# A product that begins inside the attention in front of it: three attentions of a three-block kernel on one Trainium2 core

## The chip, the cores and the metric

The kernel runs on one core of a Trainium2 chip. The engines are TensorE (PE, matmuls; PEld its weight loads), VectorE (DVE), ScalarE (ACT), GpSimd (POOL) and SyncE (SP, which issues most DMAs). The metric is the device time in microseconds; before the change the median of three runs is 1748.19 us (1746.01 to 1751.26).

## The reference

Batch 1, 512 tokens, width 1024. A first block, then a second block of two layers; in all three there is an attention whose output, gated, goes through a 1024 × 1024 product:

```python
# first block ("layer 0" in the change's words): differential attention, 8 heads
y_attn = rms_norm(diff_attention(q, k, v, lam)) @ w_attn_branch
y_mem  = memory_cross_attention(q_m, rms_norm(mem, norm_mem), w_mem_kv) @ w_mem_branch
mix = gates[0] * y_attn + gates[1] * y_pool + gates[2] * y_mem
x = x + rms_norm(mix @ w_out);  x = x + rms_norm(convolved_gated_ffn(x))
# second block, even layer: 16 heads over 512 tokens + 256 context tokens
y_lat = concat([oa * silu(ag), ob * silu(bg)]) @ ev_w_out
# second block, odd layer: a conformer convolution (31 taps, layer norm) beside
# neighbourhood attention of 8 heads
y_lat = concat([conv * silu(cg), od * silu(dg)]) @ od_w_out
```

Every matrix product is made in three matmuls of rounded halves (high × high, high × low, low × high), which gives close to float32.

## The kernel before

Activations lie with features on the partitions, as eight blocks of 128 × 512 (high halves `h`, low halves `l`). A `Product` (L451) is one output tile: 128 output features, with `kt` steps (8 for a width of 1024), each three matmuls (`mm3`, L446) over one block k of the input. Its weights come by one DMA on SP's queue (`load`), one cast on ScalarE (`whi`) and one subtraction on VectorE (`wlo`).

Products are kept in batches in one queue. `step(batch)` (L343) does the next step of the product that is current, whichever batch it is of, and takes the next product when one is done; `fetch` loads weights ahead. What is called later in time on the other engines is put off by `defer(us, fn)`: a clock of planned TensorE microseconds (`on_pe`, `tick`) says when it is emitted. TensorE's instructions stay in the order in which they are emitted; those of the other engines may be moved by the framework's scheduler, by their readiness.

An attention is a list of items, each scores, transposes ("turns") and, for every second one, an output; `attention` (L637) strings them with a lead of two or three items, and between its functions steps of a batch are put: `weave` (L406) with a fixed number per function, `pace` (L422) with so many that the batch ends with the items. The three places:

- Layer 0: `weave` at L1037 puts steps of the batches in the queue (`diffs`, the queries, keys and values of the heads, then `gates0`, three gate products) between the functions, 2.4 each (`DR`), until `gates0` is done. Then `steps(branches, KD)` (L1039) does the eight steps of the next product, gate 3 (`branch_gate(32, 3)`), `flush()` emits what is put off, and the batch `branches` goes on with branch 0 (`w_ab`, reading the attention's output `ao`, one head per block), gate 4, branch 1 and so on. Beside them runs `modulation(1, ...)`, weight rows on VectorE (L863).
- Second attention, L1603 to L1620: the filler (query and gate products) is woven with 0.5 steps per function (`LR`), one less for each product (`LZ`), 4 at once at the start; sixteen steps (`LA`) come ahead of it. Each pair of heads gives one block of `mix`: `lat_apply` multiplies it with its gate, and 2.5 us later (planned) it is split. The PSUM banks are 1 for products and 3 for the attention during the items, 2 and 2 after (`set_banks`). The product `outs` (L1612) comes after `run(filler)` and `flush()`; its result is added to `x` (`residual`), which is loaded again there (`open_x`).
- Last attention, L1819 to L1830: `pace` with gate, convolution and head products; blocks 4 to 7 of `mix` are from the attention (`na_gated`), 0 to 3 from the convolution (`conv_gated`), whose taps run on VectorE in the background. `outs` (L1824) is made after `pace`.

The memory's root: the sum of squares of `mem` is reduced by a matmul, the inverse root computed by nine small instructions on VectorE (`rsqrt`), and a matmul broadcasts it (`spread`), `gap` planned us after the sums (`SumSq.rms`, L591, called at L783). It scales the memory's keys and values when they leave PSUM (`rooted`, L705).

Of the kernel before, what the change touches and what calls it, by code (L numbers as in the profile page):

```python
# [42 lines left out]
LA, LR, LZ = 16, 0.5, 1.0  # L43
# [158 lines left out]
def body(nc, tc, A, out, dbg=None):  # L202
# [98 lines left out]
    def flush():  # L301
        while deferred:
            heapq.heappop(deferred)[2]()
# [39 lines left out]
    def step(batch):  # L343

        if current[0] is None:
            if not ahead:
                fetch()
            if batch.pulled and not batch.left:
                return END
            if not ahead[0].ready():  # L350
                return True
            ahead[0].parts()
            ahead[0].low()
            current[:] = [ahead.pop(0), 0]
        p, k = current
        fetch()
        last = k == p.kt - 1
        current[:] = [None, 0] if last else [p, k + 1]
        p.batch.steps -= 1
        p.step(k)  # L360
        if last:
            p.batch.left -= 1
            fetch()
        tick()
# [57 lines left out]
    def pace(items, lead, batch):  # L422

        left = sum(1 + len(turns) + len(late) for _, turns, late in items)
        woven.append(batch)
        for _ in attention(items, lead, True):
            left -= 1
            while batch.steps > per(batch, left) and step(batch) is None:
                pass
        woven.pop()  # L430

    def per(batch, left):

        if not hasattr(batch, "share"):
            batch.share = batch.steps / (left + 1)
        return batch.share * left
# [14 lines left out]
    class Product:  # L451
# [8 lines left out]
        adds = False  # L460

# [321 lines left out]
    defer(SM, lambda: mss.rms(roots, gap=9))  # L783
# [164 lines left out]
    def diff_item(hd, i):  # L948
# [37 lines left out]
        def output():  # L986
# [14 lines left out]
            def scaled(r):  # L1001
                V.scalar_tensor_tensor(out=of, in0=of, scalar=sub8, in1=r, op0=ALU.mult, op1=ALU.mult)
                hs = slice(half * C, half * C + C)
                split(of, ao.h[:, hd, hs], ao.l[:, hd, hs])

# [28 lines left out]
    branches = Batch(p for m in range(KD) for ps in ([branch_gate(32, m + 3)] if m < 5 else []) +  # L1034
                     [branch(32, "w_ab", m, ao, KD, lambda *a: mixed_branch(*a))] for p in ps)
    steps(diffs, DA)
    weave(attention([diff_item(hd, i) for hd in range(8) for i in range(4)], 2, True), gates0, DR)  # L1037
    run(gates0)
    steps(branches, KD)  # L1039
    flush()  # L1040
    dbg("ao", f32(ao.h))
# [548 lines left out]
    def lat_apply(m, sg):  # L1590
        V.tensor_tensor(out=mixf[:, m, :], in0=mixf[:, m, :], in1=sg, op=ALU.mult)
        defer(2.5, lambda: split(mixf[:, m, :], mix.h[:, m, :], low(m)))

    lat = Gated(lat_apply)
# [4 lines left out]
    def lat_items(n):  # L1599
# [3 lines left out]
    filler = Batch(chain(el.queries(1), lat_gate(0), lat_gate(1), when(lambda: 3 in el.qd, el.queries(2)), lat_gate(2),  # L1603
                         when(lambda: 7 in el.qd, el.queries(3)), *(lat_gate(m) for m in range(3, 8))))
# [7 lines left out]
    outs = Batch(p for m in range(KD) for p in lat_out(m))  # L1612
# [3 lines left out]
    weave(attention([it for n in range(16) for it in lat_items(n)], LL, True), filler, LR, LZ, 4)  # L1616
    run(filler)
    flush()
    set_banks(2, 2)
# [28 lines left out]

    advance(outs, 0.1)
    xst, x, xs = open_x(xd)  # L1650
    run(outs)
# [90 lines left out]
    def na_gated(m, sg):  # L1742

        V.tensor_tensor(out=grid(sg), in0=blocked(mixf[:, 4 + m, :]), in1=grid(sg), op=ALU.mult)
        split(sg, mix.h[:, 4 + m, :], low(4 + m))

# [5 lines left out]
    def conv_gated(m, sg):  # L1752
        V.scalar_tensor_tensor(out=sg, in0=sg, scalar=0.5, in1=mixf[:, m, :], op0=ALU.mult, op1=ALU.mult)
        split(sg, mix.h[:, m, :], low(m))

    conv = Gated(conv_gated, 1)
# [65 lines left out]
    pace([it for hd in range(8) for it in na_items(hd)], LN, filler)  # L1822
    wos, wop, ss = ExitStack(), [], SumSq(T)
    outs = Batch(by_halves([A["od_o"][m] for m in range(KD)], mix, lambda *a: last_out(*a), TH, lambda: wop[0]))  # L1824
# [49 lines left out]
```

## Time and profile before

| | |
|---|---|
| median of 3 runs | 1748.19 us |
| the profiled execution | 1751.09 us |
| its span | 1749.3 us, mean granted clock 0.982 |
| TensorE busy | 1658.3 us, 95% |
| VectorE busy | 1310.8 us, 75% |
| ScalarE busy | 882.0 us, 50% |
| chain that ended last | TensorE 74%, VectorE 17%, ScalarE 3% |

The profile is of one execution; times in it are microseconds from the span's start. The memory's root lies at 41 to 58 us, layer 0's attention ends at about 476, the second attention at about 1382, the last one at about 1690. A row of a timeline is one instruction (or several alike); what stands in brackets is how long its engine stood idle before it and which instruction released it. In a row of the windows view a granted clock of 1.00 is 2.4 GHz throughout, 0.50 is 1.2 GHz.

### The profile page before, as it was taken

To read this page: it belongs to the slowest core of one execution; us is meant where nothing else is said; L and a number is where in the kernel's file an instruction comes from. 1 tells how busy PE (TensorE), PEld (TensorE's weight loads), DVE (VectorE), ACT (ScalarE), POOL (GpSimd) and SP (SyncE) were. 2 spreads that over 40 slices of the span, in tenths; PEclk is the share of its full clock that TensorE was granted. 3 is DMA by queue.
4 is the path that set the end of the run, shared out by engine and by line. 5 is a ranking of instruction groups with operands and counts; after the bars stand their busy time and mean duration, and the time that the engine had idled before them with its cause. 6 is when DMAs were issued, how large, how long until landed. Compare 5 with 4: busy or idle time off the path is not lost.

```text
span 1749.3 us, 24877 instructions
## 1 busy us (share of the span) xinstructions
PE 1658.3 (95%) x8712; PEld 1389.5 (79%) x8712; DVE 1310.8 (75%) x2669; ACT 882.0 (50%) x1660; POOL 179.4 (10%) x229
## 2 busy tenths in 40 slices
PE   8999999999999989999999999899988899999898
PEld 6878878888787878888888778777877787888777
DVE  7967776777599587754874777678888665999984
ACT  6452224555433456654673343347777544554462
POOL 0120000000000000010000000013222101233200
PEclk9999999999999989999999999899999899999998
DMA  5345555444275343333332555342232346444131
GB/s 197 117 143 180 173 178 156 123 118 132 73 255 187 122 137 98 126 112 124 101 105 97 198 178 168 132 121 73 61 85 61 127 145 186 123 125 115 61 120 61
DMA packets 84876, 227.07 MB, mean 130 GB/s; under 512 B 12048, under 2 KB 24720, under 8 KB 84752
## 3 DMA queue, kind: packets, MB, share of 16 engines
q1 hardware_dynamic: 81728, 219.46, 40.5%
q10 hardware_dynamic: 3024, 6.03, 1.1%
q8 instruction: 69, 1.13, 0.3%
q14 instruction: 55, 0.45, 0.1%
HBM read 181.93 MB, written 9.44 MB: 109 GB/s over the span
## 4 chain that ended last, share of the span: by engine, by line
PE 74%; DVE 17%; ACT 3%; issue 3%; DMA 2%; POOL 0%; SPq 0%; DVEq 0%; ACTq 0%; POOLq 0%
PE mm L286 62%; PE tr L286 6%; PE s L286 4%; DVE mixf L1782 3%; PE tr L612 3%; DVE wlo L483 2%; DVE ptl L519 2%; DVE sb L1177 1%; ACT sb L1181 1%; DVE mj L863 1%; ACT whi L476 1%; DMA cb<-in_cond 1%; DMA raw<-in_ev_w 1%; DVE sqa L578 1%; DVE x L1489 1%
## 5 line engine op out<-in xcount | busy, mean ns | idle before, releaser
L286 PE MATMUL mm<-hh,whi 128*128 128x512 f32 (+1 forms) x1472 | 584.0, 397 | 19.9 <-ACT whi L476 7.2
L286 PE MATMUL mm<-hh,wlo 128*128 128x512 f32 (+1 forms) x1472 | 563.3, 383 | 9.6 <-DVE wlo L483 9.6
L286 PE MATMUL mm<-hl,whi 128*128 128x512 f32 (+1 forms) x1472 | 563.0, 382 | 1.2 <-DVE hl L1052 1.2
L476 ACT CAST whi<-raw 128x1024 fp32r<-128x1024 f32 (+2 forms) x264 | 268.7, 1018 | 343.7 <-PE mm L286 275.8
L483 DVE TENSOR_TENSOR wlo<-raw,whi 128x1024 fp32r<-128x1024 f32 (+2 forms) x264 | 311.7, 1181 | 89.1 <-PE mm L286 71.5
L286 PEld LDWEIGHTS mm<-hh,wlo 128*128 128x128 f32 x1472 | 281.1, 191 | 69.5 <-DVE wlo L483 13.2
L286 PEld LDWEIGHTS mm<-hh,whi 128*128 128x128 f32 x1472 | 282.3, 192 | 66.4 <-ACT whi L476 9.0
L286 PEld LDWEIGHTS mm<-hl,whi 128*128 128x128 f32 x1472 | 282.7, 192 | 45.3 <-DVE hl L1052 2.5
L1186 POOL TENSOR_SCALAR sb<-sb,l 128x256 f32<-128x256 f32 (+3 forms) x128 | 124.5, 973 | 971.8 <-DVE l L1185 867.8
L518 ACT CAST pth<-tr 128x512 fp32r<-128x512 f32 (+2 forms) x240 | 101.1, 434 | 95.8 <-PE tr L612 93.5
L519 DVE TENSOR_TENSOR ptl<-tr,pth 128x512 fp32r<-128x512 f32 (+2 forms) x240 | 115.7, 496 | 28.9 <-ACT pth L518 26.8
L612 PE MATMUL tr<-c,sb 128*128 128x128 f32 x624 | 105.3, 277 | 21.6 <-DVE ptl L519 13.8
L612 PEld LDWEIGHTS tr<-c,sb 128*128 128x128 f32 x624 | 78.0, 143 | 48.6 <-issue 10.8
L863 DVE CUSTOM_DVE_ANT_0 mj<-mraw,cb 128x1024 f32<-128x1024 f32 x88 | 107.5, 1222 | 0.7
L1782 DVE SCALAR_TENSOR_TENSOR mixf<-up,vec,mixf 128x512 f32<-128x512 f32 x120 | 92.0, 768 | 0.5
L286 PE MATMUL s<-kp,qd 128*128 128x256 f32 (+3 forms) x320 | 76.2, 336 | 0.7 <-ACT sb L1181 0.7
L1181 ACT ACTIVATE sb<-sb,mn 128x512 f32<-128x512 f32 (+1 forms) x64 | 49.8, 778 | 45.0 <-DVE mn L1177 36.3
L286 PE MATMUL mm<-ffh,whi 128*128 128x512 f32 x176 | 70.3, 400 | 1.1 <-ACT ffh L518 1.1
L286 PE MATMUL mm<-ffl,whi 128*128 128x512 f32 x176 | 69.9, 397 | 0.2 <-DVE ffl L519 0.2
L286 PE MATMUL mm<-ffh,wlo 128*128 128x512 f32 x176 | 69.7, 396 | 0.0
L968 ACT ACTIVATE sb<-sb,mn 128x128 f32<-128x128 f32 (+3 forms) x64 | 35.5, 556 | 54.8 <-DVE mn L966 45.4
L286 PE MATMUL mm<-mixh,whi 128*128 128x512 f32 (+1 forms) x168 | 58.8, 350 | 0.9 <-DVE mixf L1218 0.9
(382 smaller groups left out, 2699.1 us busy)
## 6 DMA issues: line engine op xcount, KB each, us to landing
raw<-in_w_in SPq DMA_DIRECT2D x56, 512.0 KB, 3.6
mraw<-in_mod_w SPq DMA_DIRECT2D x48, 512.0 KB, 4.0
raw<-in_w_up SPq DMA_DIRECT2D x44, 512.0 KB, 3.4
raw<-in_ev_w SPq DMA_DIRECT2D x40, 512.0 KB, 3.4
raw<-in_od_w SPq DMA_DIRECT2D x36, 512.0 KB, 3.4
qd<-hl SPq DMA_DIRECT2D x48, 256.0 KB, 5.0
raw<-in_w_d SPq DMA_DIRECT2D x16, 512.0 KB, 3.4
raw<-in_ev_o SPq DMA_DIRECT2D x16, 512.0 KB, 3.3
```

The source lines that it names most:

```text
L286: on_pe(nc.tensor.matmul(ps, l, r, start=start, stop=stop), max(n * 0.00042, 0.107) * (2 if l.dtype == F32 else 1))
L476: S.copy(out=self.hi[:, :n], in_=self.raw[:, :n])
L483: V.tensor_tensor(out=self.lo[:, :n], in0=self.raw[:, :n], in1=f32(self.hi[:, :n]), op=ALU.subtract)
L518: S.copy(out=hi, in_=src)
L519: V.tensor_tensor(out=lo, in0=src, in1=f32(hi), op=ALU.subtract)
L578: V.tensor_tensor(out=acc, in0=acc, in1=sq, op=ALU.add)
L612: on_pe(nc.tensor.transpose(out=ps[:, k * P:(k + 1) * P], in_=src(b), identity=ident), 0.107)
L863: tc.keep_in_program_order(V.tensor_tensor_reduce(out=jk, in0=raw, in1=cb[:, n, :], scale=0.5, scalar=0.0, op0=ALU.mult, op1=ALU.add, accu ...
L968: S.activation(out=sb[:, c, :n], in_=sb[:, c, :n], func=AF.Exp, scale=-1.0, bias=mn[:, c:c + 1], accum_out=l[:, c:c + 1])
L1181: S.activation(out=sb, in_=src, func=AF.Exp, scale=-1.0, bias=mn, accum_out=l[:, 0:1])
L1186: G.tensor_scalar(out=sb, in0=sb, scalar1=l[:, 0:1], scalar2=0.0, op0=ALU.mult, op1=ALU.add)
L1782: V.scalar_tensor_tensor(out=u[m], in0=up[:, j:j + T], scalar=wc(j), in1=u[m], op0=ALU.mult, op1=ALU.add)
```

## The change

- A product may have a `hold`: `step` does nothing while the block that its next step needs has not been planned yet.
- Layer 0: `branches` instead of `gates0` is woven between the items. Branch 0 holds at block k until both halves of head k are written; its last block waits until all put-off work is emitted.
- `pace` takes a second batch, `then`, and `more` steps: the steps of both are spread evenly over the functions, and the second batch begins when the first is done. The second attention uses it in place of `weave`, the last one with the second batch too; `more` is 7 in both, `outs` holds at a block until its split is emitted (`mixed`). In the second attention the bank change comes after the product that is current.
- The gap of the memory's root is 13 instead of 9.
- `step` looks first whether its batch is done.

```diff
-LA, LR, LZ = 16, 0.5, 1.0
+LA = 16
...
     def step(batch):
 
+        if batch.pulled and not batch.left:
+            return END
...
         p, k = current
+        if p.hold and not p.hold(k):
+            return True
...
-    def pace(items, lead, batch):
+    def pace(items, lead, batch, then, more):
 
         left = sum(1 + len(turns) + len(late) for _, turns, late in items)
+        share = (batch.steps + more) / left
         woven.append(batch)
         for _ in attention(items, lead, True):
             left -= 1
-            while batch.steps > per(batch, left) and step(batch) is None:
-                pass
+            while batch.steps + more > share * left:
+                if batch.steps:
+                    if step(batch) is not None:
+                        break
+                elif step(then) is None:
+                    more -= 1
+                else:
+                    break
         woven.pop()
...
+    def up_to_mixed(products, mixed):
+
+        products = list(products)
+        products[0].hold = lambda k: k in mixed
+        return Batch(products)
...
-    defer(SM, lambda: mss.rms(roots, gap=9))
+    defer(SM, lambda: mss.rms(roots, gap=13))
...
                 split(of, ao.h[:, hd, hs], ao.l[:, hd, hs])
+                written.append((hd, half))
...
+    written = []
+    branches[1].hold = lambda k: len(written) > (2 * k + 1 if k < KD - 1 else 2 * KD)
+    branches = Batch(branches)
     steps(diffs, DA)
-    weave(attention([diff_item(hd, i) for hd in range(8) for i in range(4)], 2, True), gates0, DR)
+    weave(attention([diff_item(hd, i) for hd in range(8) for i in range(4)], 2, True), branches, DR)
     run(gates0)
     steps(branches, KD)
     flush()
+    written.append("all")
...
-        defer(2.5, lambda: split(mixf[:, m, :], mix.h[:, m, :], low(m)))
-
+
+        def parts():
+            split(mixf[:, m, :], mix.h[:, m, :], low(m))
+            mixed.add(m)
+        defer(2.5, parts)
...
-    outs = Batch(p for m in range(KD) for p in lat_out(m))
+    outs = up_to_mixed(chain(*(lat_out(m) for m in range(KD))), mixed)
     ss = SumSq(T)
     steps(filler, LA)
     set_banks(1, 3)
-    weave(attention([it for n in range(16) for it in lat_items(n)], LL, True), filler, LR, LZ, 4)
+    pace([it for n in range(16) for it in lat_items(n)], LL, filler, outs, KD - 1)
     run(filler)
     flush()
-    set_banks(2, 2)
...
-
-    advance(outs, 0.1)
     xst, x, xs = open_x(xd)
+    while current[0]:
+        step(outs)
+    set_banks(2, 2)
     run(outs)
...
         split(sg, mix.h[:, 4 + m, :], low(4 + m))
+        mixed.add(4 + m)
...
         split(sg, mix.h[:, m, :], low(m))
-
+        mixed.add(m)
...
-    pace([it for hd in range(8) for it in na_items(hd)], LN, filler)
     wos, wop, ss = ExitStack(), [], SumSq(T)
-    outs = Batch(by_halves([A["od_o"][m] for m in range(KD)], mix, lambda *a: last_out(*a), TH, lambda: wop[0]))
+    outs = up_to_mixed(by_halves([A["od_o"][m] for m in range(KD)], mix, lambda *a: last_out(*a), TH, lambda: wop[0]), mixed)
+    pace([it for hd in range(8) for it in na_items(hd)], LN, filler, outs, KD - 1)
```

## Rows read from the trace of the kernel before

**Rows 1.** section 1 of the page: engine, busy us, share of the span, instructions

```profile
PE 1658.3 (95%) x8712; PEld 1389.5 (79%) x8712; DVE 1310.8 (75%) x2669; ACT 882.0 (50%) x1660; POOL 179.4 (10%) x229
```

**Rows 2.** windows; columns: stretch, its length, busy us (instructions) per engine, granted clock, DMA

```profile
54.00:58.00 4.00, 3.86 (x12) 3.27 (x13) 3.19 (x5) 0.37 (x1) 3.13 (x3) 0.57 0.00 0
463.00:471.00 8.00, 7.38 (x28) 6.56 (x28) 2.31 (x11) 1.01 (x3) 0.00 (x0) 0.57 0.12 47
1370.00:1386.00 16.00, 11.64 (x50) 9.22 (x49) 9.63 (x24) 9.27 (x26) 1.49 (x2) 0.68 0.48 145
1651.00:1656.00 5.00, 4.81 (x16) 4.03 (x17) 5.00 (x10) 0.27 (x1) 1.38 (x1) 0.66 0.07 28
...
1680.00:1690.00 10.00, 7.49 (x38) 5.53 (x37) 10.00 (x19) 8.18 (x17) 0.00 (x0) 1.00 0.01 2
```

**Rows 3.** timeline of TensorE, layer 0's attention: start, us, line, operation, [idle before, releaser]

```profile
458.33 0.48 PE L286 MATMUL mm<-hh,whi 128*128 128x512 f32 x1
...
461.98 0.63 PE L612 MATMUL tr<-c,sb 128*128 128x128 f32 x4 [1.21 <-ACT sqa L574]
...
475.78 0.48 PE L286 MATMUL mm<-aoh,whi 128*128 128x512 f32 x1
...
481.49 0.39 PE L286 MATMUL mm<-hh,whi 128*128 128x512 f32 x1
```

**Rows 4.** timeline of TensorE, the memory's root

```profile
54.14 1.04 PE L286 MATMUL tr<-c,rs_y 128*128 128x128 f32 x4 [2.62 <-DVE rs_y L562]
```

**Rows 5.** windows of VectorE: stretch, length, busy us (instructions), clock, DMA share, GB/s

```profile
51.00:58.50 7.50, 6.20 (x15) 0.77 0.21 70
58.50:81.00 22.50, 22.05 (x37) 1.00 0.43 141
478.00:490.00 12.00, 5.83 (x7) 1.00 0.99 363
...
500.00:554.00 54.00, 53.77 (x91) 1.00 0.61 196
1677.00:1694.00 17.00, 16.29 (x27) 1.00 0.14 44
```

**Rows 6.** timeline of VectorE, end of the second attention

```profile
1381.28 0.42 DVE L1218 TENSOR_TENSOR mixf<-tr,ot 64x256 f32<-64x256 f32 x1 [2.01 <-ACT ot L1217]
...
1383.11 0.69 DVE L519 TENSOR_TENSOR mixf<-mixf,mixh 128x512 fp32r<-128x512 f32 x1 [0.68 <-ACT mixh L518]
...
1390.84 0.74 DVE L1069 SCALAR_TENSOR_TENSOR x<-mm,mres,x 128x512 f32<-128x512 f32 x1
```

**Rows 7.** timeline of ScalarE and its queue (ACTq), behind layer 0's attention

```profile
477.41 0.83 ACTq L852 DMA_DIRECT2D cb<-in_cond  x2
...
484.26 1.06 ACT L856 ACTIVATE mj<-cb 128x1024 f32<-128x1024 f32 x1 [1.76 <-DMA cb<-in_cond]
```

**Rows 8.** timeline of TensorE, end of the second attention

```profile
1373.07 0.33 PE L612 MATMUL tr<-c,sb 128*128 128x128 f32 x1 [2.16 <-DVE ptl L519]
...
1381.75 0.80 PE L286 MATMUL mm<-mixh,whi 128*128 128x512 f32 x1 [0.91 <-DVE mixf L1218]
...
1389.16 0.39 PE L286 MATMUL mm<-mixh,whi 128*128 128x512 f32 x1
```

**Rows 9.** timeline of the SP queue, the second and the last attention

```profile
1382.17 3.75 SPq L632 DMA_DIRECT2D x<-xd  x8
...
1656.42 33.94 SPq L466 DMA_DIRECT2D raw<-in_od_o  x4
```

**Rows 10.** timeline of TensorE, end of the last attention

```profile
1686.42 0.44 PE L612 MATMUL tr<-c,sb 128*128 128x128 f32 x2 [1.91 <-DVE ptl L519]
...
1696.42 0.50 PE L286 MATMUL mm<-mixf,whi 128*128 128x512 f32 x1 [0.85 <-DVE mixf L519]
...
1696.99 0.40 PE L286 MATMUL mm<-mixh,whi 128*128 128x512 f32 x1
```

**Rows 11.** timeline of VectorE, end of the last attention

```profile
1689.88 0.68 DVE L519 TENSOR_TENSOR mixf<-cg,mixh 128x512 fp32r<-128x512 f32 x1
```

More of the change, by code (lines that the diff above doesn't have):

```diff
@@ L427, in pace @@
             left -= 1
-            while batch.steps > per(batch, left) and step(batch) is None:
-                pass
+            while batch.steps + more > share * left:
[6 more added lines that the diff above has]
+                    break
         woven.pop()
[L432 to L436, printed above, removed]
+    def up_to_mixed(products, mixed):
+        products = list(products)
+        products[0].hold = lambda k: k in mixed
+        return Batch(products)
     def need(ready):
@@ L460, in body @@
         adds = False
+        hold = None
         def load(self):
@@ L1033, in body @@
     dp = pool(dst, "dp")
-    branches = Batch(p for m in range(KD) for ps in ([branch_gate(32, m + 3)] if m < 5 else []) +
-                     [branch(32, "w_ab", m, ao, KD, lambda *a: mixed_branch(*a))] for p in ps)
+    branches = list(p for m in range(KD) for ps in ([branch_gate(32, m + 3)] if m < 5 else []) +
+                    [branch(32, "w_ab", m, ao, KD, lambda *a: mixed_branch(*a))] for p in ps)
+    written = []
+    branches[1].hold = lambda k: len(written) > (2 * k + 1 if k < KD - 1 else 2 * KD)
+    branches = Batch(branches)
     steps(diffs, DA)
-    weave(attention([diff_item(hd, i) for hd in range(8) for i in range(4)], 2, True), gates0, DR)
+    weave(attention([diff_item(hd, i) for hd in range(8) for i in range(4)], 2, True), branches, DR)
     run(gates0)
@@ L1591, in lat_apply @@
         V.tensor_tensor(out=mixf[:, m, :], in0=mixf[:, m, :], in1=sg, op=ALU.mult)
-        defer(2.5, lambda: split(mixf[:, m, :], mix.h[:, m, :], low(m)))
+        def parts():
+            split(mixf[:, m, :], mix.h[:, m, :], low(m))
+            mixed.add(m)
+        defer(2.5, parts)
+    mixed = set()
     lat = Gated(lat_apply)
@@ L1601, in lat_items @@
         return el.items(n, lambda half: mixf[64 * e:64 * e + 64, n // 2, half * C:(half + 1) * C], lambda: lat.output(n // 2))
-    filler = Batch(chain(el.queries(1), lat_gate(0), lat_gate(1), when(lambda: 3 in el.qd, el.queries(2)), lat_gate(2),
-                         when(lambda: 7 in el.qd, el.queries(3)), *(lat_gate(m) for m in range(3, 8))))
+    filler = Batch(list(chain(el.queries(1), lat_gate(0), lat_gate(1), when(lambda: 3 in el.qd, el.queries(2)), lat_gate(2),
+                              when(lambda: 7 in el.qd, el.queries(3)), *(lat_gate(m) for m in range(3, 8)))))
     def lat_out(m):
@@ L1754, in conv_gated @@
         split(sg, mix.h[:, m, :], low(m))
+        mixed.add(m)
+    mixed = set()
     conv = Gated(conv_gated, 1)
```

## The prediction

> **What bounds it now.** I read the page first: TensorE is busy for 95% of the span [rows 1], so the kernel is a TensorE kernel in the mean, and what is to be had is TensorE's idle time and its slow time. The windows view has the granted clock beside the busy times: it is 1.00 nearly everywhere, and four of its dips lie where the change works [rows 2]. A share of 0.57 over 8 us means that part of them ran at 1.2 instead of 2.4 GHz; what that costs is (1 − share) × length, if TensorE is busy. Then the timelines of TensorE around each dip, for the wait ahead of it, and those of VectorE, ScalarE and the SP queue for what that wait hangs on.
>
> The accounting is the same at each place. TensorE's work stays what it is, only its order changes. So the gain is the idle time and slow time that go, less the idle and slow time that come, and less what another engine doesn't let through. One step of a 512-column product (three matmuls) is 0.714 us: eight of them lie between 475.78 and 481.49 [rows 3].
>
> **Memory root, 9 to 13.** The broadcast of the memory's root stands in TensorE's order ahead of matmuls that don't need it, and waits 2.62 us for the last instruction of the root on VectorE [rows 4]. The clock falls right there: (1 − 0.57) × 4 = 1.72 us [rows 2]. The 4 us more of planned time put about six steps (4.3 us) ahead of it, more than the wait, so both go: 4.34 us gross. What is late next is VectorE: it has 7.5 − 6.20 = 1.30 us idle up to 58.5 and 22.5 − 22.05 = 0.45 us up to 81 [rows 5]. The low halves of the memory weights are made in that second stretch, so if they have no lead, TensorE can pull ahead by no more than 1.75 us. In the trace it never waits for them there, so there is some lead. Value 2.4, bounds 1.75 and 4.34. A loss is excluded: the root is first needed behind the first memory product, and that one comes later still.
>
> **Layer 0's attention.** The filler `gates0` runs out with the step at 458.33; behind it the last head's items wait for their transposes, 1.21 us at one place and 8 − 7.38 = 0.62 us in the dip [rows 2, 3], and the clock costs (1 − 0.57) × 8 = 3.44 us. Gross 5.27 us. In the changed order 2.4 steps follow each of the last items: the eight of gate 3 and then the first of branch 0, which may go up to block 6, because heads 0 to 6 are long written. No instruction is added. The moved steps take one weight load on SP's queue and two casts (whi on ScalarE, wlo on VectorE) along into the tail; VectorE is half idle there (5.83 of 12 us just behind it [rows 5]), so I cost them at nothing; if that cover were gone, one wlo would come on top. What comes: the last head's root, scaling and split were covered by gate 3 and branch 0, and now only by the branch's last four steps. The nearest row for such a last block is the second attention's, where from the last output to the low half 1383.11 + 0.69 − 1381.28 = 2.52 us pass [rows 6]; zero is the other end; I take 1.2, since the sums and the root still lie beside steps. That leaves 4.1. Then VectorE: from 500 to 554 it is busy for 53.77 of 54 us with the modulation's products [rows 5], so a lead of TensorE alone is handed back there. That work starts when the condition has landed, and its load is issued by ScalarE's queue right behind the last head, at 477.41; ScalarE waits for it until 484.26 [rows 7]. Seven steps (5.0 us) that came behind the last head now lie ahead of it, so it ends only 5.27 − 5.0 = 0.3 us earlier by the gross, and if the modulation alone sets the pace, that is the lower bound. But VectorE also has 6.2 us idle between 478 and 490 [rows 5], into which the evacuation and wlo of one more product fall (some 2 to 3 us by estimate). Value 3.6, nearer to TensorE's side, bounds 0.3 and 5.27.
>
> **The second attention (the latent one).** Its filler ends ten items before the end. From there to the first step of the product: waits of 2.16 and 0.91 us [rows 8]; in the whole stretch 1370 to 1386 TensorE idles 16 − 11.64 = 4.36 us, and the clock costs (1 − 0.68) × 16 = 5.12 us [rows 2]. Gross 9.48 us, up to 1389.16, where the product's second tile begins [rows 8]. Of its 14 products of 8 steps, 16 steps run ahead of it, and its heads have 216 items, so the share per item is (96 + 7) / 216 = 0.48 steps against 0.5 less one per finished product before: in the middle nothing much moves, and seven steps now lie in the last fifteen items. What comes: (a) idle that the steps don't fill, since the last items are a chain over three engines: I take 1.0 (0 to 2); (b) the last block, 2.52 us [rows 6], for which no step is left as cover, because all seven have gone by then; (c) the second tile of the product: the banks are handed over after the first one, which may make it wait for the first one's evacuation. That needs x, whose eight loads SP issues from 1382.17 on, behind eight others [rows 9], and on VectorE it stood behind other work until 1390.84 [rows 6], 1.7 us behind the end of the tile. 0 if the new bank is another one, up to 3 if x is late; I take 1.0; (d) the clock: 2.5 us idle and more just before is like the wait of 2.62 that was followed by a dip [rows 2, 4]: 1.7 to 3.4, I take 2.0. Sum 6.5, so 3.0 is left; bounds 9.48 − 2.52 = 7.0 and 9.48 − 2 − 2.52 − 3 − 3.44 = −1.5.
>
> **The last attention (neighbourhood).** Here the bound is VectorE, 16.29 of 17 us [rows 5]. TensorE's waits are 1.91 and 0.85 us [rows 10]. The filler's share grows from 195/104 to 202/104 steps per item, so it ends 3.6 items early, and blocks 0 to 6 follow. But a block is set free when its split is planned, not when it is done: the convolution's block 3 has its low half only at 1689.88 + 0.68 [rows 11]. In the new order that block's step stands ahead of the last transposes and the last output, so attention itself waits behind it; then the last block (2.5 us) has no cover, where today seven steps cover all but 0.85. The weights' loads gain nothing by the earlier place of the product: SP issues the first at 1656.42 already, as buffers come free [rows 9]. Goes: 2.76. Comes: 2.5 for the last block, about 1 in front of block 3, and a clock that may fall (I take 0.3 of 1.7, the dip at 1651 [rows 2]; the wait of 1.91 left it at 1.00 [rows 2, 10]). Value −1.0, bounds +2.1 (the 2.76 less VectorE's 0.7 of idle time [rows 5], which is all that it can catch up) and −6.0.
>
> What the Trainium skill says on this order (PSUM — Partial Sum Buffer, "Engine vs sequencer instructions"): matmuls start and complete in program order, so nothing overtakes a step that waits for its block. The trace agrees: behind the wait of 0.85 us the next matmuls start only after it, at 1696.99 [rows 10]. By that rule the third rival below is possible.
>
> **Sum.** 2.4 + 3.6 + 3.0 − 1.0 = 8.0 us. The profiled execution took 1751.09 us (span 1749.3 and 1.8 around it), so it would take 1743.1. It lies 2.9 above the median of 1748.19, at the upper edge of the three runs; the savings are differences, so I take them from the median: 1740.2, forecast 1740. The shift of the order of checks in `step` changes no instruction.
>
> **Rivals.** (1) Everything is covered: no clock falls at the new waits and VectorE hands nothing back: 4.3 + 4.1 + 7.0 + 1.0 = 16.4, 1732 us. For it: VectorE's idle time behind layer 0's attention; against: its 98% and more in the stretches behind the first two places [rows 5]. (2) Handed back: root 1.75, layer 0 0.3, the latent attention 1.0 (bank wait and a long dip of its own), the last −1.0: 2.05, 1746 us. For it: the last block's 2.5 us stand bare at two places. The Trainium skill (TensorE: Matmul & The Clock Gate, "HAM oscillation — how this bites in real kernels") advises to run all K tiles of an output in a row rather than to wait among them, so that the array stays warm; the change does the reverse and splits off the last tile, so by that rule the dips only move, and this rival's 1746 holds; the dip behind 2.62 us [rows 2, 4] agrees with it. (3) Slower: in the last attention a step that waits for a convolution block holds up the transposes and the output queued behind it on TensorE. Price: 4 us for blocks 1 to 3, 2.5 for the last block, 3.4 of clock, less 2.76: −7.1; with root and layer 0 at their lower bounds (2.05) and −1.5 at the latent one, 6.5 slower, and 1755 us. It decides from about 4 us of such waits in front of the last output. For it: VectorE has no room there [rows 5] to make the blocks sooner; against it: part of these waits falls where TensorE waits today (1.91 us [rows 10]). (4) The change doesn't do what it says: the blocks come free so late that the product begins no earlier, and only the root gains: 1746 us.
>
> **Chances.** Forecast 0.55 (its own range 1735 to 1745), everything covered 0.17, handed back 0.16, slower 0.07, no early start 0.05. A measurement of this kernel can tell 0.3%, 5.2 us, from no change: faster means under 1743. From the forecast 0.43, all of (1) and some 0.03 of (2) and (4) lie there: 0.63; slower 0.06, the rest 0.31. The range for 8 in 10 cuts the far tails of (1) and (2), and most of (3): 1731 to 1748.
>
> **What would show it.** Right: no wait before the memory's root, and clock 1.00 from 54 to 58; at 458 to 476 steps of gate 3 and the branch between the last head's transposes, clock 1.00, the matmul of block 7 about 1.2 us behind its predecessor, and the modulation's end on VectorE 0.3 to 5 us earlier; in the latent attention seven steps among the last fifteen items, a wait of 2.5 us before block 7 with a dip behind it; in the last one waits of a step for a mix block before the last output. Wrong: dips at the old places, a wait of TensorE on the modulation stage that is longer by what was won, or a second tile of the latent product that waits for over 3 us.

## The result, and the profile after

The changed kernel takes 1765.3 us (median of four runs, 1763.8 to 1769.2), the kernel before 1748.1 (four runs): ratio 1.0099, 95% interval 1.0085 to 1.0114. It is slower by 17 us where 8 us of gain were forecast. The profiled executions differ by less, 12.7 us (spans 1762.0 and 1749.3), because the one of before lies 3.0 us above its median and the one of after is the fastest of its four. Section 1 of the page after: TensorE's work is the same [rows 1], only the span is longer.

```profile
PE 1655.8 (94%) x8712; PEld 1389.5 (79%) x8712; DVE 1312.9 (75%) x2669; ACT 883.2 (50%) x1660; POOL 178.2 (10%) x229
```

To find the place, I took from both traces the starts of the same instructions of TensorE and compared the time between them. The stages end at the first score matmul of layer 0 (before: 273.8 us), the first `tr<-c,ta` (629.4), the first `mm<-c,tg` behind the second attention (1448.6) and the last instruction; the end of the last `mm<-mh,wlo` (1103.6) cuts off the second attention's stage.

| stage | forecast | after − before |
|---|---|---|
| memory root | −2.4 | −3.9 |
| layer 0's attention | −3.6 | −0.5 |
| between (unchanged) | 0 | −0.5 |
| second attention | −3.0 | +8.3 |
| last attention to the end | +1.0 | +9.3 |

So up to 1100 us the changed kernel leads by 4.8 us, of 6.0 forecast; the two later attentions lose 17.6 where 2.0 were to be won. In the other kernels below, stages that they leave alone come out within 0.8 us of before in some two cases of three, up to 4.2 off where clock dips fall differently. A stage compares one profiled execution with one, so where it and a ratio differ (by up to 3.4 us) the ratio is the safer of the two.

**Where it goes.** Mostly into idle time: in the second attention's stage TensorE is idle for 36.4 us after and 29.2 before, in the last one for 29.3 and 21.4. The waits view of TensorE over the second attention, kernel before (who waits, for whom: us in total, times, longest):

```profile
PE tr L612 <- DVE ptl L519: 9.3, 10, 2.2
PE tr L286 <- DVE ptl L519: 6.0, 8, 1.3
PE tr L612 <- DVE l L1185: 3.6, 3, 1.7
```

and the kernel after, where `tg` is what ScalarE writes when it empties a filler product's bank, and `x` is the residual, which empties the output product's:

```profile
PE mm L286 <- ACT tg L637: 8.0, 5, 2.9
PE mm L286 <- DVE x L1087: 5.6, 1, 5.6
PE mm L286 <- ACT tg L1119: 4.6, 3, 2.4
PE tr L624 <- DVE ptl L531: 3.9, 4, 1.9
PE mm L286 <- ACT mixh L530: 2.3, 1, 2.3
```

The three groups of waits shown for before, 18.9 us, have shrunk to 6.0 (3.9, 1.2 and 0.9), as wanted. In their place the first matmul of a product waits eight times, 12.6 us in all, for `tg`; before, no such wait was longer than 0.13 us. The longest of them, 2.9 us at 1366.7, is that of the output product itself, which begins behind the last filler product in the same bank. Another one, TensorE's timeline of after:

```profile
1213.13 0.39 PE L286 MATMUL mm<-hh,wlo 128*128 128x512 f32 x1
...
1216.57 0.50 PE L286 MATMUL mm<-hh,whi 128*128 128x512 f32 x1 [2.39 <-ACT tg L1119]
```

and ScalarE meanwhile:

```profile
1213.33 1.06 ACT L488 CAST whi<-raw 128x1024 fp32r<-128x1024 f32 x1 [0.79 <-PE mm L286]
1214.29 0.84 ACT L530 CAST pth<-tr 128x512 fp32r<-128x512 f32 x2
1215.02 0.91 ACT L1199 ACTIVATE sb<-s,mn 128x768 f32<-128x768 f32 x1
...
1215.91 0.60 ACT L1119 ACTIVATE tg<-mm 128x512 f32<-128x512 f32 x1
```

The product is complete at 1213.5. Its evacuation is 0.60 us of work, but it stands behind a weight cast, two casts and an exponential. During this attention there is one bank for products (`set_banks(1, 3)`), so the next product cannot begin before 1216.5. The wait for `x` at the end of the stage:

```profile
1384.43 0.51 PE L286 MATMUL mm<-mixh,wlo 128*128 128x512 f32 x1
1390.52 0.76 PE L286 MATMUL mm<-mixh,whi 128*128 128x512 f32 x1 [5.58 <-DVE x L1087]
```

The first output tile is done at 1384.9, and the second waits 5.58 us, until VectorE has done what stands ahead of the residual, and the residual itself:

```profile
1384.98 1.23 DVE L495 TENSOR_TENSOR wlo<-raw,whi 128x1024 fp32r<-128x1024 f32 x1 [0.94 <-PE mm L286]
1386.12 3.59 DVE L590 TENSOR_TENSOR sqb<-sqb,ta 128x256 f32<-128x256 f32 x7
1389.63 0.75 DVE L1087 SCALAR_TENSOR_TENSOR x<-mm,mres,x 128x512 f32<-128x512 f32 x1
```

The clock, windows of after (columns as in [rows 2]; the clock is the third figure from the right): the dips at 54 and in layer 0's attention are gone, and the two later attentions have new ones behind the new waits; the dip at the end of the second attention is still there.

```profile
54.00:58.00 4.00, 4.00 (x21) 3.31 (x20) 3.92 (x8) 3.39 (x6) 2.49 (x3) 1.00 0.13 29
...
458.00:476.00 18.00, 16.99 (x89) 13.93 (x89) 9.65 (x29) 6.03 (x11) 0.00 (x0) 1.00 0.51 176
...
1170.00:1186.00 16.00, 12.42 (x65) 10.51 (x64) 14.69 (x27) 9.39 (x19) 4.54 (x4) 0.79 0.23 61
1208.00:1224.00 16.00, 13.41 (x76) 11.42 (x75) 10.53 (x20) 8.58 (x20) 3.81 (x5) 0.89 0.26 68
...
1380.00:1396.00 16.00, 7.90 (x26) 5.82 (x27) 6.92 (x13) 5.14 (x12) 0.00 (x0) 0.68 0.75 247
1686.00:1696.00 10.00, 7.03 (x32) 5.69 (x31) 10.00 (x19) 7.36 (x15) 1.42 (x1) 0.83 0.01 2
1704.00:1712.00 8.00, 5.87 (x22) 4.21 (x22) 5.78 (x7) 4.24 (x6) 0.00 (x0) 0.80 0.67 202
```

In the last attention the longer waits are for VectorE. TensorE's waits from 1500 to 1712 us, the largest of them, before and then after:

```profile
PE tr L612 <- DVE ptl L519: 4.5, 4, 1.9
PE tr L612 <- DVE mixf L1808: 0.5, 1, 0.5
```

```profile
PE tr L624 <- DVE ptl L531: 6.9, 3, 2.5
PE tr L624 <- DVE mixf L1834: 3.0, 1, 3.0
PE mm L624 <- ACT tg L1100: 2.6, 3, 1.0
```

### The profile page after: what moved, and what is told of

The parts are those of the page before. It is cut to its first block, busy times and chain, and to the rows that moved or that the text cites. A ratio compares the mean times of both kernels' runs of the same rounds, so it can differ in the third digit from the quotient of the medians.

```text
span 1762.0 us, 24867 instructions
## 1 busy us (share of the span) xinstructions
PE 1655.8 (94%) x8712; PEld 1389.5 (79%) x8712; DVE 1312.9 (75%) x2669; ACT 883.2 (50%) x1660; POOL 178.2 (10%) x229
## 4 chain that ended last, share of the span: by engine, by line
PE 74%; DVE 18%; ACT 3%; issue 3%; DMA 2%; POOL 0%; SPq 0%; DVEq 0%; ACTq 0%; POOLq 0%
PE mm L286 61%; PE tr L286 6%; DVE mixf L1808 4%; PE s L286 3%; PE tr L624 3%; DVE wlo L495 3%; DVE ptl L531 1%; DVE mj L875 1%; DVE sb L1195 1%; ACT sb L1199 1%; ACT whi L488 1%; DVE x L1507 1%; DVE mn L1193 1%; ACT pth L530 1%; DMA cb<-in_cond 0%
## 5 line engine op out<-in xcount | busy, mean ns | idle before, releaser
L1204 POOL TENSOR_SCALAR sb<-sb,l 128x256 f32<-128x256 f32 (+3 forms) x128 | 120.0, 938 | 997.6 <-DVE l L1203 663.1
```

The costliest lines, as they stand in the source:

```text
L1204: G.tensor_scalar(out=sb, in0=sb, scalar1=l[:, 0:1], scalar2=0.0, op0=ALU.mult, op1=ALU.add)
```

## The experiments

Ratios are to the kernel before, run on the same chip with them; intervals are 95%. "Stage" is the stage's time against before, from the traces. Of an edit its main lines are shown, against the kernel before or against the run that is named with it.

**One part alone.** Four kernels, each with one part of the change.

> Of the whole change only the memory root is 4 us later. Theory: in the trace of the changed kernel TensorE leads by 3.9 us behind this place, loses 1.6 of it to a clock dip that comes at 104 us, and has it back when the dip of before at 259 us is missing; nothing behind it takes the lead. So the whole lead stays: 1748.1 - 3.9 = 1744 us. Rival: VectorE's saturated modulation stage at 500 to 554 us gives it back, as it does with layer 0's lead; then the end moves by less than 1.5 us, 1747 us or more.

```
-    defer(SM, lambda: mss.rms(roots, gap=9))
+    defer(SM, lambda: mss.rms(roots, gap=13))
```

0.9979 (0.9963 to 0.9996): 3.7 us gained. The stage gains 3.8, and layer 0's stage, where the rival had VectorE give it back, comes out at 0.0 against before, as the theory had it; the interval alone would leave room for the rival.

> Only layer 0's attention is changed (the branch products are its filler, with the hold on blocks). Theory: TensorE begins the branch product 9 us earlier than before and ends it 4 us earlier, and VectorE's modulation stage hands it back, so that behind 629 us 0.5 us is left: 1747.6 us. Rival: that the handing back in the changed kernel came only because the root's lead of 3.9 us was already taken from the same VectorE time; alone, this edit then keeps 3 to 4 us: 1744.5 us.

```
-    weave(attention([diff_item(hd, i) ...], 2, True), gates0, DR)
+    branches[1].hold = lambda k: len(written) > (2 * k + 1 if k < KD - 1 else 2 * KD)
...
+    weave(attention([diff_item(hd, i) ...], 2, True), branches, DR)
```

1.0010 (0.9998 to 1.0021), the stage −0.45. The theory holds, the rival (3 to 4 us) falls.

> Only the second (latent) attention is changed: even pace, the product begun inside, banks handed over later. Theory: this part costs 8.3 us by itself, the difference of the two traces between 1103 and 1457 us: about 8 us of waits of a product's first matmul for ScalarE's gate evacuation (one bank for products, and the pause behind each product is gone), 5.6 us for the second output tile, less the 9.5 us that it was to save, plus clock dips: 1756.4 us. Rival: the loss comes from the phase in which the earlier parts put this stage (clock, DMA); alone it gains what was forecast, 3 us: 1745 us.

```
-    weave(attention([... lat_items(n)], LL, True), filler, LR, LZ, 4)
+    pace([... lat_items(n)], LL, filler, outs, KD - 1)
```

1.0071 (1.0052 to 1.0091), the stage +9.0. The loss is this part's own.

> Only the last (neighbourhood) attention is changed: share of the filler 202 instead of 195 steps over the same items, product begun inside. Theory: this part costs 9.3 us by itself, the difference of the two traces from 1457 us to the end: VectorE is saturated, so a filler that is denser by 3.6% puts some four items of attention behind it, and they come out as a bare tail: 1757.4 us. Rival: it is the shift inherited from the second attention (another phase of the weights' loads and of the clock) that costs here; alone it costs about 1 us, as forecast: 1749 us.

```
-    pace([... na_items(hd)], LN, filler)
+    pace([... na_items(hd)], LN, filler, outs, KD - 1)
```

1.0059 (1.0036 to 1.0082), the stage +10.7. Also its own. Together: −0.0021 + 0.0010 + 0.0071 + 0.0059 = +0.0119, beside +0.0099 for the whole change; the parts add up within their intervals.

**The second attention: pause, density, early product.**

> The second attention alone, as in the run before (1761.3 us), but with a pause of two items behind each finished product of the filler. Theory: the waits of a product's first matmul for ScalarE's evacuation of the only product bank (13.7 us of waits for tg in eight places) come from the dropped pause; with it they fall below 3 us and the kernel gains 8 to 11 us, 1751 to 1753 us. Rival 1: the bank is not the point, ScalarE is too full for the even pace; the waits move to the attention's own transposes and less than 3 us are gained, 1758 us or more.

Against e3_second:

```
             left -= 1
+            if idle:
+                idle -= 1
+                continue
             while batch.steps + more > share * left:
                 if batch.steps:
                     if step(batch) is not None:
                         break
+                    if rest and current[0] is None:
+                        idle = rest
+                        break
...
-    pace([... lat_items(n)], LL, filler, outs, KD - 1)
+    pace([... lat_items(n)], LL, filler, outs, KD - 1, 2)
```

1.0022 (1.0007 to 1.0037), the stage +1.1 instead of +9.0; the waits for `tg` are 6.1 us in four places instead of 13.7 in eight. The gain is in the range of the theory (8.6 us by the ratios, 8 to 11 expected): the dropped pause had given the evacuation its time. But the waits only halve; they don't fall below 3 us.

> Only the filler of the second attention is spread evenly by the new pace (96 steps over 216 items, no pause behind a product); the output product begins behind the attention, in two banks, as before. Theory: the waits for tg stay (10 us or more) and the waits at the end of attention are replaced by filler steps: 1752 to 1756 us, so the pace loses by itself. Rival: the pace alone is harmless (within 2 us of before, 1750 us) and the loss of this part comes from beginning the product early.

```
-    weave(attention([... lat_items(n)], LL, True), filler, LR, LZ, 4)
+    pace([... lat_items(n)], LL, filler, None, 0)
```

0.9973 (0.9959 to 0.9987), the stage −6.5. My theory falls, and the rival, nearer, doesn't say enough: the even pace alone (4.7 us by the ratio) is worth more than the whole part was forecast at. Its waits over the second attention:

```profile
PE tr L624 <- DVE ptl L531: 6.5, 8, 1.7
PE mm L286 <- ACT tg L637: 2.4, 2, 1.8
PE mm L286 <- ACT tg L1113: 2.4, 3, 1.7
```

There is no pause here either, and only 4.8 us of waits for `tg`. So the pause may be one way to give the bank its time, and fewer steps per item another. That made the share itself a suspect, 96 or 103 steps over the same 216 items; against e8_second_pace_only:

> Only the second attention: the new pace at the changed share (103 steps over 216 items instead of 96), no pause behind a product, but the output product begins behind the attention, in two banks. Theory: 0.48 instead of 0.44 steps per item is what brings the waits for the only product bank (13.7 us of them at 0.48 with the early product, 4.8 us at 0.44 without); the waits come back here and with them 4 to 9 us over the pace alone: 1748 to 1753 us. Rival: the density is harmless, and what the early product does (its handover, its bare last block) is the whole loss; then it is within 2 us of the pace alone, 1743 to 1746 us.

```
-    pace([... lat_items(n)], LL, filler, None, 0)
+    pace([... lat_items(n)], LL, filler, None, KD - 1)
```

0.9998 (0.9982 to 1.0013), the stage +0.2: 6.7 us more than with 96. The waits for `tg` are 10.7 us in seven places:

```profile
PE tr L624 <- DVE ptl L531: 6.5, 6, 2.2
PE mm L286 <- ACT tg L637: 6.1, 4, 2.7
PE mm L286 <- ACT tg L1113: 4.6, 3, 2.4
```

The theory holds, near its lower end by the ratios (4.4 us; 4 to 9 expected). What is left from here to e3_second, 8.8 us by the stages and 12.8 by the ratios, is the early product. Three waits come with it: 2.9 us of its first matmul for the only bank, 2.3 of its last block, 5.7 of the second tile. The next kernels are about the last of these.

> The second attention alone, and when the banks are handed over behind the first output tile, the second tile takes the other bank. Theory: the wait of 5.68 us of the second tile is one for the bank that the first tile still holds; it goes, and with it some of the clock dip behind it: 5 to 7 us better than the run without it, 1754.5 to 1756.5 us. Rival: the second tile has to wait anyway (weights, or x), or the third tile waits in its place for the residual, which VectorE starts 5 us late; then less than 2 us, 1759.5 us or more.

> The second attention alone, with both: the pause behind each product and the other bank for the second tile. Theory: the two waits are the whole loss (13.7 and 5.7 us of waits with their dips), so it comes to the 3 us of gain that were forecast for this stage, or a little more: 1743 to 1747 us. Rival: the last block's bare wait (2.3 us) and the clock leave nothing of the gain: 1749 us or more.

The same line, in e6_second_bank against e3_second, in e7_second_rest_bank against e5_second_rest:

```
     while current[0]:
         step(outs)
     set_banks(2, 2)
+    mmps()
```

1.0053 (1.0038 to 1.0068) and, with the pause, 1.0007 (0.9995 to 1.0019). In both the wait stays (5.63 and 5.68 us), and neither kernel comes to the time of its theory. By my reading of the program these two say nothing of the bank: a tile that nobody writes takes no place, so the second tile still lay in the first one's bank. No view shows where a tile lies; the kernels below bear it out.

> The second attention with the pause behind each product, the product begun inside and the other bank for the second tile, as in the run that came to 1752.5 us; here the pools of PSUM banks hand over bank by bank (a new tile waits only for the readers of its own bank) instead of as a whole. Theory: the 5.7 us wait of the second tile is one for the handover of the whole pool, whose last reader is the residual of the first tile on VectorE; it goes, and 4 to 7 us with it: 1746 to 1748.5 us. Rival: the tile waits for something else that VectorE does late, and the wait stays: 1751 us or more.

Against e7_second_rest_bank:

```
-        banks.update(st=st, p=pool(st, "pm", space=PS), mm=mm, tr=tr)
+        banks.update(st=st, p=pool(st, "pm", space=PS, reuse_waits="tile"), mm=mm, tr=tr)
```

1.0009 (0.9990 to 1.0027); 5.59 us of wait. By the same reading it is inconclusive.

> As the run with the pause and the other bank (0.999 to 1.002 of before), but now the first bank of the new pair is taken up by one written element, so that the second tile of the product really lies in the other bank; in the two runs that meant to do this it still lay in the first tile's bank. Theory: the second tile's wait of 5.7 us is for that bank (its reader is the residual of the first tile on VectorE), so it falls below 1 us, the next tile waits under 1 us, and 4 to 7 us are gained: 0.997 of before. Rival: what VectorE does late is needed in any case, and the wait moves to the third tile; less than 2 us are gained.

Against e7_second_rest_bank:

```
-    mmps()
+    V.memset(mmps()[:, 0:1], 0.0)
```

1.0009 (0.9996 to 1.0022). Now the tile lies in the other bank by that reading, and the wait is still 5.59 us: in the program TensorE's queue has a wait for the residual ahead of it, for the new pool as a whole. (The waits view puts it down to the one written element, which VectorE did right behind the residual, at 1391.80. But the trace also has a wait for VectorE in TensorE's queue, ahead of the matmul; it ends at 1391.76, when the residual is done, at 1391.72, and the one element not begun.) Neither the other bank alone nor the handover bank by bank alone removes it.

> The second attention with the pause and the early product; the second tile lies in the other bank, as in the run before this one, and the PSUM pools hand over bank by bank, so that it waits for the old readers of that bank only. In the run before it lay in the other bank and still waited 5.6 us, since the new pool as a whole waited for the last reader of the old one, the residual of the first tile. Theory: the wait of 5.6 us goes, the third tile waits under 1 us in its place, and 4 to 7 us are gained: 0.997 to 0.9985 of before. Rival: something else that comes late (the weights' casts, x) holds the second or third tile, and less than 2 us are gained: 1.000 or more.

Against e5_second_rest:

```
-        banks.update(st=st, p=pool(st, "pm", space=PS), mm=mm, tr=tr)
+        banks.update(st=st, p=pool(st, "pm", space=PS, reuse_waits="tile"), mm=mm, tr=tr)
...
+    V.memset(mmps()[:, 0:1], 0.0)
```

0.9978 (0.9965 to 0.9991), the stage −5.7: with both edits the wait is gone. TensorE's timeline, the last block of the first tile and the second tile behind it:

```profile
1382.14 0.49 PE L286 MATMUL mm<-mixh,whi 128*128 128x512 f32 x1 [2.29 <-ACT mixh L537]
...
1383.20 0.55 PE L286 MATMUL mm<-mixh,wlo 128*128 128x512 f32 x1
1383.55 0.63 PE L286 MATMUL mm<-mixh,whi 128*128 128x512 f32 x1
```

The theory is confirmed, with 6.7 us against e5_second_rest, within 4 to 7 (7.7 by the ratios). Of the four kernels without and with either edit only this one has no wait, so it takes both. And yet the early product, mended twice, only reaches the even pace without it (−5.7 and −6.5): the last block's 2.29 us and a dip behind it (a matmul takes 0.63 us in the last row) stand bare, as they were priced. Its share is still 103, though, so the two kernels differ in more than this; the early product at 96 was not run.

**The last attention: density alone, both ways.**

> Only the last attention: the filler at the changed share (202 instead of 195 steps over the 104 items), but the output product begins behind the attention as before. Theory: the density alone does the damage, since VectorE is saturated and the attention falls some four items behind; so nearly the whole 10 us of that part: 1756 to 1759 us. Rival: beginning the product inside does it (its last block stands bare); then the density alone is within 2 us of before, 1749 us.

```
-    pace([... na_items(hd)], LN, filler)
+    pace([... na_items(hd)], LN, filler, None, KD - 1)
```

1.0053 (1.0035 to 1.0071), the stage +10.0 of the 10.7: the density does it (with it, that the filler ends 3.6 items early). Nothing of the early product is in this kernel, and its waits are those of the changed one:

```profile
PE tr L624 <- DVE ptl L531: 8.3, 4, 2.5
PE tr L624 <- DVE mixf L1820: 3.0, 1, 3.0
PE mm L624 <- ACT tg L1094: 2.6, 3, 1.0
```

> Only the last attention, the other way: the filler at 188 instead of 195 steps over the 104 items, so that seven steps of it are left behind the attention. Theory: if a denser filler puts attention behind, a sparser one puts it ahead by four items; the last output comes earlier and seven steps cover it: 2 to 6 us gained, 1743 to 1747 us. Rival: the share of before is a balance, and TensorE waits as much for attention's VectorE work with fewer steps between the items; then it is within 2 us of before or slower.

```
+    pace([... na_items(hd)], LN, filler, None, 1 - KD)
```

1.0054 (1.0034 to 1.0073), the stage +9.4. My theory falls: fewer steps lose as much. TensorE now waits for the attention itself, 9.4 us in three places, one of them 5.1:

```profile
PE tr L624 <- DVE ptl L531: 9.4, 3, 5.1
```

Counted in the traces by what starts at 1640 us or later, 38 filler steps and 28 transposes of the attention (`tr<-c,sb`) are still to come before, 39 and 36 in the dense order, 44 and 28 in the sparse one. The dense order is no further with the filler and behind with the attention, the sparse one no further with the attention and behind with the filler. Windows, kernel before and then the dense one (busy us: TensorE, its loads, VectorE, ...):

```profile
1600.00:1650.00 50.00, 46.56 (x245) 37.21 (x244) 49.87 (x93) 24.04 (x47) 12.20 (x10) 1.00 0.32 90
1650.00:1700.00 50.00, 44.96 (x232) 36.47 (x233) 44.09 (x82) 27.06 (x50) 5.03 (x4) 0.97 0.29 100
```

```profile
1600.00:1650.00 50.00, 42.13 (x225) 34.48 (x223) 49.46 (x88) 21.39 (x43) 13.36 (x10) 1.00 0.37 102
1650.00:1700.00 50.00, 43.06 (x224) 35.55 (x223) 40.87 (x85) 27.60 (x54) 5.59 (x5) 0.91 0.16 53
```

Up to 1650 VectorE is full in both, and TensorE gets 4.4 us less through; behind it VectorE is busy 3.2 us less, and the granted clock is 0.91 where it was 0.97 (3.0 us of 50). What is left there is a chain of attention items with little filler beside it; that this is why VectorE idles is argued, not tested.

> Only the last attention, its filler at 197 instead of 195 steps over the 104 items (1.89 instead of 1.875 a item; the changed kernel has 1.94). Theory: the loss goes with the density, so two sevenths of the 9 us that 202 cost: 1.5 to 4 us slower than before, 1.001 to 1.002. Rival: the order of before is a lucky one, and any other share loses as much as 188 and 202 did (both 1.005): 8 us or more.

```
+    pace([... na_items(hd)], LN, filler, None, 2)
```

1.0013 (1.0001 to 1.0026), the stage +1.6. So on the dense side the loss grows with the distance from the share of before; it is not a cliff. On the sparse side there is one point, and shares just below 195 were not run.

**What is worth keeping.**

> The two parts that gained alone, together: the memory root 4 us later, and the second attention's filler in the even pace at 96 steps over 216 items, its product begun behind the attention. Theory: the two places don't share a bound, so the gains add: 0.9979 x 0.9973 = 0.9952 of the kernel before, 1740 us. Rival: the root's lead is lost in the second attention's clock dips, as 1.6 us of it once were at 104 us; then no better than the pace alone, 0.9973.

```
-    defer(SM, lambda: mss.rms(roots, gap=9))
+    defer(SM, lambda: mss.rms(roots, gap=13))
...
-    weave(attention([... lat_items(n)], LL, True), filler, LR, LZ, 4)
+    pace([... lat_items(n)], LL, filler, None, 0)
```

0.9949 (0.9931 to 0.9968): they add, as the theory had it; the rival's 0.9973 lies outside.

> As the first of these runs (root and even pace at 96 steps, product behind the attention), with a pause of two items behind each finished product of the filler. Theory: of the 4.8 us of waits for the only product bank that the pace at 96 has left, 3 go: 0.9935 to 0.995 of before. Rival: the catching up behind the pause makes as much wait elsewhere: within 0.1% of the first of these runs.

Against f1_root_pace:

```
-    pace([... lat_items(n)], LL, filler, None, 0)
+    pace([... lat_items(n)], LL, filler, None, 0, 2)
```

0.9941 (0.9920 to 0.9963), 1738.7 us: the fastest, but not to be told from the run ahead of it. The time fits theory and rival. Its waits for `tg` decide: they are unchanged (4.8 us, of which 3 were to go), so the pause brings nothing at this share.

> As the fastest run so far (root, even pace at 96 with the pause: 0.9941), and layer 0's attention of the change with it. Theory: VectorE's modulation stage hands layer 0's lead back, so the part is worth at most the 1 us that its trace showed alone: 0.993 to 0.9945. Rival: with the root's lead in front of it, it costs the 1 us that its times alone showed (1.001), or more: 0.995 or more.

Against f4_root_pace_rest:

```
+    branches[1].hold = lambda k: len(written) > (2 * k + 1 if k < KD - 1 else 2 * KD)
...
-    weave(attention([diff_item(hd, i) ...], 2, True), gates0, DR)
+    weave(attention([diff_item(hd, i) ...], 2, True), branches, DR)
```

0.9946 (0.9925 to 0.9967). Layer 0's part adds nothing that can be measured.

## Why the prediction was wrong

**Memory root: right, the size low.** The broadcast has no wait any more and the clock is 1.00 from 54 to 58. It measured 3.9 us in the stage (3.7 by the ratio of e1_root), not 2.4: VectorE did not take the lead back as the value assumed; it lies in the bounds (1.75 to 4.34).

**Layer 0: the mechanism right, the value wrong by 3 us.** The dip is gone, the last block waits 1.01 us (1.2 forecast), and with this part alone TensorE leads by 4.8 us more in the branch product than ahead of this stage. Then 4.4 of it go again, most of it in waits for VectorE, which is full in its modulation stage (44.3 of the 45 us from 500 to 545): 0.8 us at a weight's low half and 2.2 at a broadcast. TensorE's timeline, after:

```profile
531.11 0.50 PE L286 MATMUL mm<-aoh,wlo 128*128 128x512 f32 x1 [1.48 <-DVE wlo L495]
...
548.82 1.19 PE L286 MATMUL tr<-c,rs_y 128*128 128x128 f32 x4 [3.76 <-DVE rs_y L574]
```

and before, where the same two waited 0.68 and 1.55:

```profile
539.02 0.50 PE L286 MATMUL mm<-aoh,wlo 128*128 128x512 f32 x1 [0.68 <-DVE wlo L483]
...
554.52 0.68 PE L286 MATMUL tr<-c,rs_y 128*128 128x128 f32 x4 [1.55 <-DVE rs_y L562]
```

The rest, some 1.4 us, goes to a clock dip behind the longer wait, at 548 us after and at 552 in e2_layer0, which before does not have there. The same window, before and then after:

```profile
540.00:556.00 16.00, 13.65 (x62) 10.57 (x62) 14.89 (x32) 4.57 (x7) 0.00 (x0) 1.00 0.49 159
```

```profile
540.00:556.00 16.00, 11.44 (x47) 8.90 (x46) 14.41 (x35) 6.24 (x12) 0.00 (x0) 0.89 0.58 197
```

What was left, 0.45 us, is close to the lower bound of 0.3. The idle 6.2 us of VectorE ahead of that stage [rows 5] were of little use to it: choosing the value nearer to TensorE's side was the error, and no term stood for a dip behind the wait. The text's own sign of failure, a longer wait on the modulation stage, came true.

**Second attention: two terms failed.** Much of the gross gain was real: the even pace alone brought 6.5 of the 9.5 us (4.7 by the ratio). The first failed term is "in the middle nothing much moves". The text had the old rule in hand, 0.5 per item "less one per finished product", and read it as a rate. It was a pause, and at 103 steps the only bank for products needed it. The term was 0; the share of 103 instead of 96 costs 6.7 us (4.4 by the ratios), or, seen the other way, the missing pause at that share 8.0 with the early product in place. The two don't add: both are mostly the waits for that bank. More than one bank for products was not tried. The second is (c), the second tile's bank, 1.0 with bounds 0 to 3: it waited 5.6 us, and f5_second_bank_by_bank, where that wait is gone, gains 6.7. The residual's place behind other work of VectorE was seen [rows 6], but not that the pool of banks hands over as a whole, so that any tile behind the handover would wait for it. The text's own sign of failure, a second tile that waits for over 3 us, came true. Term (b), 2.52 us for the last block, measured 2.3. No term stood for the wait of the product's own first matmul for the only bank, 2.9 us.

With one bank, eight groups of matmuls, the output product's first among them, waited 12.6 us for the emptying of the group ahead of them, in the waits view of after. The Trainium skill has a rule for this that I did not weigh (Perfetto Trace Analysis, "Matmuls"): independent matmul groups should rotate through PSUM banks, so that the emptying of one lies beside the next one's matmuls. The trace agrees, by its reverse.

**Last attention: the sign right, the size and the mechanism not.** −1.0 was forecast, −9.3 came, below the bound of −6.0, for which the text gives no working. The failed step is "it ends 3.6 items early, and blocks 0 to 6 follow", which gave the denser share no price of its own. VectorE was known to be full there [rows 5], and that is why it has one: the density alone cost 10.0 us (e9_last_dense). As the counts and windows of that run have it, with VectorE full more of the filler per item left eight more transposes of the attention behind 1640 us, and these come at the end with little beside them. The third rival came nearest in time (1755 predicted for the whole, 1765 measured) and had the right stage, with 0.07; but its mechanism, a step that waits for a convolution block and holds up the transposes, did not happen. The only waits for a block are the last block's, 1.54 and 0.59 us:

```profile
1707.03 0.49 PE L286 MATMUL mm<-mixh,whi 128*128 128x512 f32 x1 [1.54 <-ACT mixh L530]
1708.12 0.50 PE L286 MATMUL mm<-mixf,whi 128*128 128x512 f32 x1 [0.59 <-DVE mixf L531]
```

**The clock** moved with the waits, as the second rival had it: the dips at 54 and 464 us went, and others came at 548, 1176, 1217, 1691 and 1708, behind new or longer waits. One at 105 us came, and one at 259 went, at waits that nobody changed.

## What to carry to other kernels

A pause in a hand-made order may be the time that a single buffer needs: before it is smoothed away, count who waits for the buffer it feeds. Where another engine is full, the ratio of main work to filler is a choice of its own: here a change of 4% to either side cost 9 to 10 us, more than the 2.76 us of waits at the end that it was to fill. Try the even spread, the share and the early start apart: here the even spread alone was worth 6.5 us, and with the denser share and the early start it became a loss of 9.0.

## What the runs showed of the hardware that was not expected

Whether a wait costs clock is not settled by its length. The wait of 2.27 us of the same matmul is followed by half clock before and not after; windows of the ten us around it, before and then after:

```profile
257.00:267.00 10.00, 9.33 (x33) 7.41 (x34) 3.11 (x6) 1.80 (x3) 0.00 (x0) 0.83 0.80 210
```

```profile
255.00:265.00 10.00, 9.66 (x44) 7.84 (x45) 3.31 (x6) 2.12 (x3) 0.00 (x0) 1.00 0.87 227
```

At a wait of 1.66 us (1.67 before) some 105 us into the span it is the other way round: 0.83 after in the ten us around it, 1.00 before. So a lead won early can lose 1.7 us or win it at a place that nobody touched; one to three such dips are the size of the differences over 0.8 us that unchanged stages show.
